# A gated encoder layer: Gelu where each block's result lies, two pairs of g_b tiles as seven products, and a DMA that makes a weight's lower part

## The chip, the cores and the metric

The kernel runs on one core of one Trainium2 chip. The metric is the time of one execution in microseconds (us) of device time. The core has five engines with instruction queues of their own that run beside each other: TensorE (PE, matrix products), VectorE (DVE), ScalarE (ACT), GpSimd (POOL) and SyncE (SP). POOL and SP also start DMA transfers from their queues. An engine takes its instructions in the order in which they stand; a waiting instruction holds up all that stand behind it.

## The reference

One layer on 512 time steps with a model width of 2048, all in float32:

```python
h = rmsnorm(x, norm_g)
v, bg, cg, za, u, zb, ga, gb = split(h @ w_in)          # widths 2048 x4, 1024 x2, 2048 x2
ya = bg * causal_depthwise_conv(cg * v, conv_w)
ya = (ya * silu(za)) @ w_out_a
yb = gelu(s5_scan(u, ...))                              # 64 groups of 16 channels, 64 states each
yb = yb * sigmoid(yb @ w_glu + b_glu)
yb = (yb * silu(zb)) @ w_out_b
m = sigmoid(ga) * ya + sigmoid(gb) * yb
out = rmsnorm(x + m @ w_o, final_g)
```

## The kernel before, in words

**Products.** Each float32 operand is held as two parts, an upper one that is rounded to the matmul's type and a lower one that is the rest; both stand in one tile `pair` for activations, in `w_hi` and `w_lo` for weights. A weight tile is 128 x 1024: eight blocks of 128 rows for 128 output columns. `gemm` (lines 828 to 836) takes one such tile and, for each block, issues three matmuls of 512 columns (lines 833 to 835): upper by upper, upper by lower, lower by upper. `hgemm` is two of them, one output tile of 128 channels by 512 steps over all 2048 rows.

**Seven products.** `seven` (lines 1082 to 1111) computes a pair of output tiles with seven products over half the rows in place of eight, from sums of weight blocks (`add7`) and sums of activations (`h_comb`). A product is 8 matmuls of 512 columns with `w_hi` (line 1073) and 8 of 256 with `w_lo` (line 1078). Of its seven weight tiles five are loaded by SP; on two of these a second load of POOL adds another block by an accumulating DMA (line 647), and two sums are DVE operations (lines 567 and 571).

**The stream of weights.** `WStream` holds a list of weight tiles in the order of use. For each, SP loads `w_raw` (line 641), ACT makes `w_hi` by a cast (`_hi`, line 663) and DVE makes `w_lo` as `w_raw - w_hi` (`_lo`, line 680). There are four buffers of `w_hi` and four of `w_lo`; `get`, called at each product, prepares those a few products ahead.

**Stages.** First u (8 tiles, with the norm). Then the gate stage: 16 g_b tiles (`gate`: a `hgemm`, Tanh on ACT, a store to `gb_d` on POOL's queue) and 8 z_b tiles, and beside them the SSM. Then GLU (8 gemms on the Gelu operands `yg`), the product with w_out_b (16 gemms; there the stored g_b tiles come back and are multiplied with the result into `tb_d`), two g_a tiles, and the stage of sevens: for j = 0, 2, ..., 14 a pair each of cg, v, z_a and b_g, and for j = 2 to 12 also a pair of g_a. At the end w_out_a, the sum m and w_o.

**The SSM beside the gates.** `ssm_blocks` is a generator over four blocks of 8 x 2 groups. Each yields pieces of work: `loads` (15 DMAs on POOL's queue: u, b and c, a broadcast table, another table), `front`, `table`, `pe1` (matmuls), `post`, `scan`, `skip`, and one block later `pe2` (matmuls) and `result` (adds the matmul's result to `ysb`, and stores it by four DMAs over u in the tile `uy`). Behind it in the list of background work stands `gelu`, which for each of eight slabs of `uy` copies it, makes the Gelu in its Tanh form and splits it into a `pair` of `yg`.

**What sets the order.** A planner, `step(n)`, is called in each gemm with a rate (5.3 in the gate stage): it takes pieces from the background list until their estimated cost has used up n. A piece that yields a number above 0 lets as many following calls pass. The language's scheduler then sets the order of each engine's queue.

Of the kernel before, what the change touches and what calls it, by code (L numbers as in the profile page):

```python
# [9 lines left out]
F32 = mybir.dt.float32  # L10
# [16 lines left out]
SLOT = 1024  # L27
EPS = 1e-6
MAGIC = 12582912.0
RATE = 5.3  # L30
PRATE = 1.6
R7 = 1.2
WARM = 9
NR4 = 37
NA = 0
NAB = 2
NB7 = 14
LEAST = 0.6
# [234 lines left out]
class Block:  # L273
# [13 lines left out]
    def loads(self):  # L287
        c, nc, b, q0 = self.c, self.c.nc, self.b, self.q0
        u4 = self.u4 = self.new([P, QB, NCH], "u4")
        for s in range(T):  # L290
            nc.gpsimd.dma_start(u4[s * 32:(s + 1) * 32], self.uy[self.rows, :, s, :])
        smal = self.smal = self.new([P, QB, 2, 2, NC], "bc")
        nc.gpsimd.dma_start(smal[:, :, 0], self.be_d[b])
        nc.gpsimd.dma_start(smal[:, :, 1], self.ce_d[b])
        wb = self.wb = self.new([P, QB, 2, NP], "wb")
        sc = self.scratch.rearrange("(q g) s r p -> s g q (r p)", g=2)
        for s in range(T):
            for g2 in range(2):
                r0 = s * 32 + g2 * 16
                nc.gpsimd.dma_start(  # L300
                    wb[r0:r0 + 16].rearrange("c q r p -> c q (r p)"),
                    sc[s, g2, q0:q0 + QB, :].unsqueeze(0).to_broadcast([16, QB, 2 * NP]))
        bs = self.bs = self.new([P, QB, 2, NP], "bs")
        nc.gpsimd.dma_start(bs, self.bs_d[b])

    def front(self):
        c, nc, b, q0, msk = self.c, self.c.nc, self.b, self.q0, self.msk
# [191 lines left out]
                yield  # L499

    def result(self):
        c, nc, ysb = self.c, self.c.nc, self.ysb
        tt, ts, stt = _ew(nc)
        for half in range(2):
            y = ysb[:, half * 4:half * 4 + 4, :].rearrange("p q k -> p (q k)")
            tt(y, self.yp[half], y, ADD)
        for t_ in range(T):
            nc.gpsimd.dma_start(self.uy[self.rows, :, t_, :], ysb[t_ * 32:(t_ + 1) * 32])
        yield


def ssm_blocks(blocks):

    blocks[0].loads()
    yield 1
    for i, k in enumerate(blocks):
        yield from k.front()
        if i:
            blocks[i - 1].pe2()
            yield  # L520
        yield from k.table((4, 5))
        if i:
            yield from blocks[i - 1].result()
        k.pe1()
        yield from k.table((6,))
        yield from k.post()
        if i + 1 < len(blocks):
            blocks[i + 1].loads()
        yield from k.scan()
        yield from k.skip()  # L530
    yield 1
    blocks[-1].pe2()
    yield 1
    yield from blocks[-1].result()


class WStream:
# [12 lines left out]

        self.loads.append((len(self.ops), len(self.ops), src, box))

    def add(self, src, resident=False, first=None):
        box = {}
        self._load(src, box)
        self.ops.append((lambda: box["x"], box, resident, first))

# [108 lines left out]
    def _lo(self):  # L666
        c, nc = self.c, self.c.nc
        i = self.nb
        if i >= len(self.ops):
            return  # L670
        while self.na <= i:
            self._hi()
        self.nb += 1
        raw, hi, cuts, resident = self.hl[i]
        if resident:
            lo = c.r4.tile([P, SLOT], F32R, tag="r4", name="w_lo_r")
        else:
            lo = c.wp.tile([P, SLOT], F32R, tag="lo", bufs=4, name="w_lo")
        for a, b in zip(cuts, cuts[1:]):
            nc.vector.tensor_tensor(out=lo[:, a:b], in0=raw[:, a:b], in1=hi.bitcast(F32)[:, a:b], op=SUB)  # L680
        self.hl[i] = (hi, lo)
# [15 lines left out]
def hybrid_kernel(ctx: ExitStack, tc: tile.TileContext, xT, x, cvec, fg, wu, wu7, wabc,  # L697
# [44 lines left out]
    for j in range(NA):  # L742
        for h in range(2):
            W.add(wga[j, h])
    for j in range(KD):
        for h in range(2):
            W.add(wgb[j, h])
    for m in range(8):
        for h in range(2):
            W.add(wgz[m, 1 + h])  # L750
# [57 lines left out]
    def step(n=1.0):  # L808

        if hold[0] > 0:
            hold[0] -= 1
            return
        owed[0] += n
        while owed[0] > 0.0 and bg:
            t = SPENT[0]
            try:
                hold[0] = next(bg[0]) or 0
            except StopIteration:  # L820
                bg.pop(0)
                continue
            owed[0] -= max(SPENT[0] - t, LEAST)
            if hold[0]:
                owed[0] = 0.0
        owed[0] = min(owed[0], n)

    def gemm(ps, acts, first=True, last=True, steps=0.0):
# [106 lines left out]

    yg = []

    def gelu(a, b):
        q = []
        for m in range(a, b + 1):  # L940
            if m < b:
                y, t = tmp(), tmp()
                act.copy(y.rearrange("p (k s) -> p k s", s=T), uy[:, m].rearrange("p s k -> p k s"))
                act.activation(t, y, AF.Square, scale=0.044715 ** 0.5)
                stt(t, t, 1.0, y, ADD, MUL)
                act.activation(t, t, AF.Tanh, scale=0.7978845608028654)
                q.append((y, t))
                yield
            if m > a:
                y, t = q.pop(0)  # L950
                stt(t, t, 1.0, y, ADD, MUL)
                g = pair()
                split(g, t)
                yg.append(g)
                yield

    bg.append(ssm_blocks([Block(c, b, uy, scratch, bs_d, be_d, ce_d, dsk, msk) for b in range(NB)]))
    bg.append(gelu(0, 8))

    def hgemm(steps=0.0):  # L960
        ps = psum()
# [10 lines left out]

    for j in range(NA):
        gate(ga_d[j // 2][:, j % 2], RATE)
    for j in range(KD):
        gate(gb_d[j], RATE)
    zb = []
    for m in range(8):
# [56 lines left out]
    gq = []  # L1035

    def fetch_gb():
        if len(gq) < KD:
            t = tmp()
            nc.gpsimd.dma_start(t, gb_d[len(gq)])  # L1040
            gq.append(t)
# [5 lines left out]
    for j in range(KD):  # L1047
        ps = psum()
        gemm(ps, yb, steps=1.15)
        th = gq[j]  # L1050
        stt(th, th, 1.0, ps, ADD, MUL)
        nc.gpsimd.dma_start(tb_d[j // 2][:, j % 2], th)
        fetch_gb()
    for j in range(NA, NAB):
# [81 lines left out]
    def gate2(o, j):  # L1136
# [384 lines left out]
```

## Time and profile before

| what | us |
|---|---|
| median of 3 runs | 1655.29 |
| the runs | 1653.54, 1655.29, 2033.42 |
| the profiled execution | 1653.86 |
| its span, first to last instruction | 1652.1 |

The profile is of one execution. Its page gives for each engine the time it was busy, the chain of work that ended last, and groups of instructions by line with their mean duration in ns and the idle time ahead of them, with what ended that idle time. "PEld" is PE's loading of weights into its array. A matmul's duration in a row is longer than its place in the chain, since neighbours overlap; the pace of PE is read from the chain. A wait is named as "engine tile line <- what released it". The DMA share is the mean busy share of the core's 16 DMA engines.

### The profile page before, as it was taken

The numbers are of one execution on the slowest core, as the hardware profiler recorded it, in microseconds if no ns is written. First come the engines' busy times: TensorE is split into PE (matmuls) and PEld (weight loads), VectorE is DVE, ScalarE is ACT, GpSimd is POOL, SyncE is SP. The second block draws the span as 40 slices with busy tenths as digits, with TensorE's granted clock in tenths as the row PEclk, the third lists the DMA queues.
The fourth block names the chain that finished last, engine by engine and source line by source line (L and its number), as shares of the span: only waits on it lengthen the run. The fifth ranks groups of instructions, "written<-read, shape, count | busy, mean of one in ns | idle before, by whom it ended". The sixth has DMA issues, their size and how long they took to land.

```text
span 1652.1 us, 22757 instructions
## 1 busy us (share of the span) xinstructions
PE 1641.3 (99%) x8636; PEld 1409.8 (85%) x8636; DVE 1290.6 (78%) x1743; ACT 788.0 (48%) x1081; POOL 220.7 (13%) x347
## 2 busy tenths in 40 slices
PE   9999999999999999999999999999999999999997
PEld 7888888888888888888888888888888888888886
DVE  8997777976766687878878787787878778888497
ACT  6433455347422454545445455544555544455334
POOL 0003233200021100010000101010010221122000
PEclk9999999999999999999999999999999999999999
DMA  8323464432454577777767777777777878897683
GB/s 310 115 86 111 121 164 132 139 119 77 167 184 150 162 186 206 193 217 186 198 191 192 216 184 208 204 208 197 187 204 191 297 255 252 269 327 249 227 327 102
DMA packets 91918, 318.50 MB, mean 193 GB/s; under 512 B 11904, under 2 KB 12160, under 8 KB 91808
## 3 DMA queue, kind: packets, MB, share of 16 engines
q1 hardware_dynamic: 58752, 204.65, 35.7%
q0 software_dynamic: 32336, 111.30, 28.6%
q8 instruction: 67, 1.10, 0.3%
q10 hardware_dynamic: 720, 1.10, 0.2%
q14 instruction: 43, 0.35, 0.1%
HBM read 287.51 MB, written 25.30 MB: 189 GB/s over the span
## 4 chain that ended last, share of the span: by engine, by line
PE 98%; DVE 1%; DMA 0%; ACT 0%; SPq 0%; issue 0%; DVEq 0%
PE ps L1073 34%; PE ps L1078 18%; PE ps L835 10%; PE ps L833 10%; PE ps L834 10%; PE ps L1296 10%; PE ps L916 1%; PE ps L917 1%; PE ps L918 1%; PE ps L375 1%; PE ps L487 1%; PE ps L383 0%; PE ps L484 0%; DMA w_raw<-in_wu_dram 0%; DVE uy L66 0%; DVE o L76 0%
## 5 line engine op out<-in xcount | busy, mean ns | idle before, releaser
L663 ACT CAST w_hi<-w_raw 128x1024 fp32r<-128x1024 f32 (+2 forms) x459 | 479.1, 1045 | 666.1 <-PE ps L1073 278.2
L680 DVE TENSOR_TENSOR w_lo<-w_raw,w_hi 128x1024 fp32r<-128x1024 f32 (+2 forms) x459 | 556.1, 1213 | 182.1 <-ACT w_hi L663 178.8
L1073 PE MATMUL ps<-h_comb,w_hi 128*128 128x512 f32 x1408 | 352.6, 392 | 0.0
L1073 PEld LDWEIGHTS ps<-h_comb,w_hi 128*128 128x128 f32 x1408 | 253.2, 189 | 45.3
L835 PE MATMUL ps<-pair,w_lo 128*128 128x512 f32 x720 | 280.6, 390 | 0.7 <-DVE w_lo L680 0.7
L833 PE MATMUL ps<-pair,w_hi 128*128 128x512 f32 x720 | 280.9, 390 | 0.0
L834 PE MATMUL ps<-pair,w_hi 128*128 128x512 f32 x720 | 280.2, 389 | 0.0
L1073 PE MATMUL ps<-pair,w_hi 128*128 128x512 f32 x1056 | 264.4, 392 | 0.0
L1073 PEld LDWEIGHTS ps<-pair,w_hi 128*128 128x128 f32 x1056 | 190.1, 189 | 34.0
L1078 PEld LDWEIGHTS ps<-h_comb,w_lo 128*128 128x128 f32 x1408 | 192.1, 190 | 13.7
L1078 PE MATMUL ps<-h_comb,w_lo 128*128 128x256 f32 x1408 | 196.3, 282 | 0.0
L835 PEld LDWEIGHTS ps<-pair,w_lo 128*128 128x128 f32 x720 | 135.2, 188 | 29.2 <-DVE w_lo L680 1.4
L834 PEld LDWEIGHTS ps<-pair,w_hi 128*128 128x128 f32 x720 | 135.2, 188 | 28.0
L833 PEld LDWEIGHTS ps<-pair,w_hi 128*128 128x128 f32 x720 | 135.2, 188 | 27.7
L1078 PEld LDWEIGHTS ps<-pair,w_lo 128*128 128x128 f32 x1056 | 144.1, 190 | 10.3
L1078 PE MATMUL ps<-pair,w_lo 128*128 128x256 f32 x1056 | 147.3, 282 | 0.0
L66 DVE TENSOR_TENSOR half<-ps,half 128x512 f32<-128x512 f32 x132 | 90.6, 686 | 67.4 <-PE ps L1078 67.4
L647 POOL DMA_DIRECT2D w_raw<-in_wabc_dram x64 | 55.1, 861 | 554.9 <-DMA w_raw<-in_wabc_dram 392.2
L1296 PE MATMUL ps<-w_hi,pair 128*128 128x512 f32 x192 | 60.7, 389 | 0.0
L567 DVE TENSOR_TENSOR w_raw<-w_raw 128x1024 f32<-128x1024 f32 x44 | 53.9, 1225 | 2.2 <-DMA w_raw<-in_wga_dram 0.7
L571 DVE TENSOR_TENSOR w_raw<-w_raw 128x1024 f32<-128x1024 f32 x44 | 53.9, 1225 | 1.5
L1296 PE MATMUL ps<-w_hi,m_half 128*128 128x512 f32 x160 | 50.7, 389 | 0.0
(215 smaller groups left out, 1718.7 us busy)
## 6 DMA issues: line engine op xcount, KB each, us to landing
w_raw<-in_wabc_dram SPq DMA_DIRECT2D x160, 512.0 KB, 4.5
w_raw<-in_wga_dram SPq DMA_DIRECT2D x76, 512.0 KB, 5.1
w_raw<-in_wabc_dram POOLq DMA_DIRECT2D x64, 512.0 KB, 6.4
w_raw<-in_wo_dram SPq DMA_DIRECT2D x52, 512.0 KB, 5.9
w_raw<-in_wgb_dram SPq DMA_DIRECT2D x48, 512.0 KB, 3.5
w_raw<-in_wgz_dram SPq DMA_DIRECT2D x24, 512.0 KB, 3.3
w_raw<-in_wga_dram POOLq DMA_DIRECT2D x24, 512.0 KB, 7.2
m_r<-m POOLq DMA_DIRECT2D x32, 256.0 KB, 5.6
```

Of the source, the lines that this page charges most:

```text
L66: return v.tensor_tensor(out=o, in0=a, in1=b, op=op)
L567: tt(out=b11["x"], in0=b11["x"], in1=s1["x"], op=ADD)
L571: tt(out=s1["x"], in0=b12["x"], in1=b11["x"], op=ADD)
L647: nc.gpsimd.dma_start(box["x"], src.rearrange("p a b -> p (a b)"), accum_op=ADD)
L663: nc.scalar.copy(hi[:, a:b], raw[:, a:b])
L680: nc.vector.tensor_tensor(out=lo[:, a:b], in0=raw[:, a:b], in1=hi.bitcast(F32)[:, a:b], op=SUB)
L833: nc.tensor.matmul(ps, hi[:, k], a[:, 0], start=first and k == 0, stop=False)
L834: nc.tensor.matmul(ps, hi[:, k], a[:, 1], start=False, stop=False)
L835: nc.tensor.matmul(ps, lo[:, k], a[:, 0], start=False, stop=last and k == 7)
L1073: nc.tensor.matmul(ps if flat else both, hi[:, k], a, start=first and k == 0, stop=False, skip_group_check=True)
L1078: nc.tensor.matmul(ps[:, HL:], lo[:, k], a[:, :HL] if flat else a[:, 0], start=False, stop=last and k == 7, skip_group_check=True)
L1296: nc.tensor.matmul(ps, l, r[:, k2, c0:c1], start=first and k2 == i == 0, stop=last and k2 == 1 and i == 2, skip_group_check=True)
```

## The change

There are four parts.

1. `WStream.add` takes `by_dma`; for the second weight tile of each g_b output tile ACT writes `-w_hi` into `w_lo` and POOL's queue starts a DMA that adds the weight from memory, in place of DVE's subtraction.
2. The g_b tiles 12 to 15 leave the gate stage. In the w_out_b stage their results are stored as they are, and after the sevens of j = 0 and j = 14 `seven` computes the pairs 12, 13 and 14, 15; `gate_b` loads the stored pair, multiplies and stores it.
3. `Block.result` makes the Gelu on its 1024 columns, in three pieces, before the store; `gelu` becomes `operands`, which only makes the pairs. The rate is 6.0, and the last block's pieces yield -1: they end the surplus that a call has left, without letting calls pass.
4. `loads` and the stores of `result` are started on SP's queue.

```diff
-RATE = 5.3
+RATE = 6.0
+NGB = 12
+GB7 = {0: 12, 14: 14}
...
     def loads(self):
-            nc.gpsimd.dma_start(u4[s * 32:(s + 1) * 32], self.uy[self.rows, :, s, :])
+            nc.sync.dma_start(u4[s * 32:(s + 1) * 32], self.uy[self.rows, :, s, :])
...
     def result(self):
-        for half in range(2):
-            y = ysb[:, half * 4:half * 4 + 4, :].rearrange("p q k -> p (q k)")
-            tt(y, self.yp[half], y, ADD)
+        y = self.ysb.rearrange("p q k -> p (q k)")
+        for half in range(2):
+            h = y[:, half * L:(half + 1) * L]
+            tt(h, self.yp[half], h, ADD)
+        t = self.new([P, QB * NCH], "gelu")
+        nc.scalar.activation(t, y, AF.Square, scale=0.044715 ** 0.5)
+        yield
+        stt(t, t, 1.0, y, ADD, MUL)
+        nc.scalar.activation(t, t, AF.Tanh, scale=0.7978845608028654)
+        yield
+        stt(y, t, 1.0, y, ADD, MUL)
         for t_ in range(T):
-            nc.gpsimd.dma_start(self.uy[self.rows, :, t_, :], ysb[t_ * 32:(t_ + 1) * 32])
+            nc.sync.dma_start(self.uy[self.rows, :, t_, :], self.ysb[t_ * 32:(t_ + 1) * 32])
...
-    yield 1
-    blocks[-1].pe2()
-    yield 1
-    yield from blocks[-1].result()
+    yield -1
+    blocks[-1].pe2()
+    yield -1
+    yield from blocks[-1].result()
+    yield 1
...
     def _lo(self):
+        if "src" in self.ops[i][1]:
+            nc.scalar.mul(lo, hi.bitcast(F32), -1.0)
+            nc.gpsimd.dma_start(lo, self.ops[i][1]["src"].rearrange("p a b -> p (a b)"), accum_op=ADD)
+            cuts = cuts[:1]
...
-    for j in range(KD):
+    for j in range(NGB):
         for h in range(2):
-            W.add(wgb[j, h])
+            W.add(wgb[j, h], by_dma=h == 1)
...
+        if j in GB7:
+            i = GB7[j]
+            W.add7(wgb[i, 0], wgb[i + 1, 0], wgb[i + 1, 1], wgb[i, 1])
...
                 hold[0] = next(bg[0]) or 0
+                if hold[0]:
+                    owed[0] = min(owed[0], 0.0)
...
-            if hold[0]:
-                owed[0] = 0.0
...
-    def gelu(a, b):
...
+    def operands():
+        for m in range(8):
+            g = pair()
+            v = uy[:, m].rearrange("p s k -> p k s")
+            act.copy(g[:, 0].rearrange("p (k s) -> p k s", s=T), v)
+            tt(g[:, 1].rearrange("p (k s) -> p k s", s=T), v,
+               g[:, 0].bitcast(F32).rearrange("p (k s) -> p k s", s=T), SUB)
+            yg.append(g)
+            yield
...
-        th = gq[j]
-        stt(th, th, 1.0, ps, ADD, MUL)
+        if j < NGB:
+            th = gq[j]
+            stt(th, th, 1.0, ps, ADD, MUL)
+        else:
+            th = tmp()
+            act.copy(th, ps)
...
+    def gate_b(o, j):
+        t, r = wide("tz"), wide("tb_w")
+        nc.gpsimd.dma_start(r, tb_d[j // 2])
+        act.activation(t, o, AF.Tanh, scale=0.5)
+        yield
+        stt(r, t, 1.0, r, ADD, MUL)
+        nc.gpsimd.dma_start(tb_d[j // 2], r)
+        yield
...
+        if j in GB7:
+            bg.append(gate_b(seven("gb", hb), GB7[j]))
```

How this moves instructions is seen at three places. The first is the start of the gate stage on POOL's queue. Before, stores of g_b tiles (L970) and the loads of the first block (L291 to L304) stand there:

```order
L970 DMA gb_112<-tmp 128x512
L970 DMA gb_113<-tmp 128x512
L291 DMA ssm_u_1336<-uy 32x8x128 x4
L970 DMA gb_114<-tmp 128x512
L293 DMA ssm_bc<-in_be_dram 128x8x32
L268 DMA ssm_scr<-ssm_wn 64x512
```

Now a load onto `w_lo` (L698) follows each store, each store now being L985:

```order
L698 DMA w_lo<-in_wgb_dram 128x1024 x2
L985 DMA gb_112<-tmp 128x512
L698 DMA w_lo<-in_wgb_dram 128x1024
L985 DMA gb_113<-tmp 128x512
L698 DMA w_lo<-in_wgb_dram 128x1024
L271 DMA ssm_scr<-ssm_wn 64x512
L985 DMA gb_114<-tmp 128x512
L698 DMA w_lo<-in_wgb_dram 128x1024
```

The accumulating loads stand behind the stores of earlier tiles, and the block's loads are gone from this queue.

The second place is SP's queue over the gate stage and what follows. Before, nothing but weight loads stands there (wgb holds g_b and w_out_b, wgz GLU and z_b, wabc and wga those of the sevens):

```order
L641 DMA w_raw<-in_wgb_dram 128x1024 x32
L641 DMA w_raw<-in_wgz_dram 128x1024 x24
L641 DMA w_raw<-in_wgb_dram 128x1024 x16
L641 DMA w_raw<-in_wga_dram 128x1024 x4
L641 DMA w_raw<-in_wabc_dram 128x1024 x40
```

Now, around the third block's loads and the first block's result (`uy<-ssm_y`, L520):

```order
L658 DMA w_raw<-in_wgb_dram 128x1024 x8
L294 DMA ssm_u_2069<-uy 32x8x128 x3
L520 DMA uy<-ssm_y 32x8x128 x4
L294 DMA ssm_u_2069<-uy 32x8x128
L296 DMA ssm_bc<-in_be_dram 128x8x32
L297 DMA ssm_bc<-in_ce_dram 128x8x32
L303 DMA ssm_wb<-ssm_scr 16x8x128 x8
L307 DMA ssm_bs<-in_bs_dram 128x1024
L658 DMA w_raw<-in_wgz_dram 128x1024 x7
```

The 15 loads and the four stores stand between two groups of weight loads.

The third place is ACT's queue at the end of the gate stage, where GLU's operands are made. Before, copies of u (L943), the Gelu's two functions (L944, L946) and the casts of the pairs (L734) mix with the casts of weights (L663):

```order
L943 COPY tmp<-uy 128x512
L944 ACTIVATE tmp<-tmp 128x512
L943 COPY tmp<-uy 128x512
L663 CAST w_hi<-w_raw 128x1024
L946 ACTIVATE tmp<-tmp 128x512
L944 ACTIVATE tmp<-tmp 128x512
L943 COPY tmp<-uy 128x512
L946 ACTIVATE tmp<-tmp 128x512
L734 CAST pair<-tmp 128x512
```

Now the last block's Gelu (L513, L516) stands two weight casts ahead of eight casts straight from u (L966):

```order
L513 ACTIVATE ssm_gelu<-ssm_y 128x1024
L516 ACTIVATE ssm_gelu<-ssm_gelu 128x1024
L680 CAST w_hi<-w_raw 128x1024
L998 ACTIVATE tmp<-ps 128x512
L680 CAST w_hi<-w_raw 128x1024
L966 CAST pair<-uy 128x512 x8
L998 ACTIVATE tmp<-ps 128x512
```

Of the work that follows the last result, the two functions for each slab are gone. On PE, 71 matmuls (23 of a z_b gemm under way and two whole gemms) stand in the new order between the last SSM matmul and the first GLU matmul.

More of the change, by code (lines that the diff above doesn't have):

```diff
@@ L290, in loads @@
         for s in range(T):
-            nc.gpsimd.dma_start(u4[s * 32:(s + 1) * 32], self.uy[self.rows, :, s, :])
+            nc.sync.dma_start(u4[s * 32:(s + 1) * 32], self.uy[self.rows, :, s, :])
         smal = self.smal = self.new([P, QB, 2, 2, NC], "bc")
-        nc.gpsimd.dma_start(smal[:, :, 0], self.be_d[b])
-        nc.gpsimd.dma_start(smal[:, :, 1], self.ce_d[b])
+        nc.sync.dma_start(smal[:, :, 0], self.be_d[b])
+        nc.sync.dma_start(smal[:, :, 1], self.ce_d[b])
         wb = self.wb = self.new([P, QB, 2, NP], "wb")
@@ L299, in loads @@
                 r0 = s * 32 + g2 * 16
-                nc.gpsimd.dma_start(
+                nc.sync.dma_start(
                     wb[r0:r0 + 16].rearrange("c q r p -> c q (r p)"),
@@ L303, in loads @@
         bs = self.bs = self.new([P, QB, 2, NP], "bs")
-        nc.gpsimd.dma_start(bs, self.bs_d[b])
+        nc.sync.dma_start(bs, self.bs_d[b])
     def front(self):
@@ L501, in result @@
     def result(self):
[L502 removed]
+        c, nc = self.c, self.c.nc
         tt, ts, stt = _ew(nc)
+        y = self.ysb.rearrange("p q k -> p (q k)")
         for half in range(2):
[L505 to L506 removed]
+            h = y[:, half * L:(half + 1) * L]
[7 more added lines that the diff above has]
+        stt(y, t, 1.0, y, ADD, MUL)
         for t_ in range(T):
[L508 removed]
+            nc.sync.dma_start(self.uy[self.rows, :, t_, :], self.ysb[t_ * 32:(t_ + 1) * 32])
         yield
@@ L517, in ssm_blocks @@
         yield from k.front()
+        res = iter(())
         if i:
@@ L520, in ssm_blocks @@
             yield
+            res = blocks[i - 1].result()
         yield from k.table((4, 5))
-        if i:
-            yield from blocks[i - 1].result()
+        next(res, None)
         k.pe1()
-        yield from k.table((6,))
+        for _ in k.table((6,)):
+            yield
+            next(res, None)
         yield from k.post()
@@ L551, in _load, with add @@
         self.loads.append((len(self.ops), len(self.ops), src, box))
-    def add(self, src, resident=False, first=None):
-        box = {}
+    def add(self, src, resident=False, first=None, by_dma=False):
+        box = {"src": src} if by_dma else {}
         self._load(src, box)
@@ L936, in hybrid_kernel @@
     yg = []
-    def gelu(a, b):
[L939 to L955, printed above, removed]
+    def operands():
[7 more added lines that the diff above has]
+            yield
     bg.append(ssm_blocks([Block(c, b, uy, scratch, bs_d, be_d, ce_d, dsk, msk) for b in range(NB)]))
-    bg.append(gelu(0, 8))
+    bg.append(operands())
     def hgemm(steps=0.0):
@@ L974, in hybrid_kernel @@
         gate(ga_d[j // 2][:, j % 2], RATE)
-    for j in range(KD):
+    for j in range(NGB):
         gate(gb_d[j], RATE)
@@ L1037, in fetch_gb @@
     def fetch_gb():
-        if len(gq) < KD:
+        if len(gq) < NGB:
             t = tmp()
@@ L1140, in gate2 @@
         yield
+    def gate_b(o, j):
[5 more added lines that the diff above has]
+        nc.gpsimd.dma_start(tb_d[j // 2], r)
+        yield
     hb = blocks(hp, th7)
```

## The prediction

> **What bounds the kernel.** I read the page first, then the waits of TensorE, the chain of waits, then each stage by windows. Times are microseconds (us). Busy time of each engine and the chain's shares, from the page:
>
> ```profile
> PE 1641.3 (99%) x8636; PEld 1409.8 (85%) x8636; DVE 1290.6 (78%) x1743; ACT 788.0 (48%) x1081; POOL 220.7 (13%) x347
> ...
> PE 98%; DVE 1%; DMA 0%; ACT 0%; SPq 0%; issue 0%; DVEq 0%
> ```
>
> A modelled busy share of 99% does not yet say that nothing waits, so the second view is what TensorE (PE) waited for, total, times, longest:
>
> ```profile
> PE ps L791 <- DVE bgl L785: 1.1, 1, 1.1
> PE ps L835 <- DVE w_lo L680: 0.7, 1, 0.7
> PE ps L916 <- ACT pair L893: 0.4, 1, 0.4
> ```
>
> That is 2.2 us in the whole execution. The change can win only what it takes out of PE's own matmuls, and lose only by making PE wait. The two stages it touches, the gate stage (g_b and z_b tiles with the SSM beside them) and the stage of seven products, by windows:
>
> ```profile
> core 0: us, PE busy (x) PEld busy (x) DVE busy (x) ACT busy (x) POOL busy (x), PEclk, DMA share, GB/s
> 95.00:403.00 308.00, 307.31 (x1608) 260.66 (x1607) 243.53 (x426) 143.04 (x240) 67.92 (x113) 1.00 0.42 124
> ...
> 554.00:1034.00 480.00, 480.00 (x2749) 422.36 (x2748) 372.75 (x380) 243.87 (x292) 47.68 (x59) 1.00 0.73 198
> ```
>
> VectorE (DVE) is at 79% and 78%, the granted clock is 1.00: PE paces both, and the others have room.
>
> **The one term of the sum: PE.** The price of a product in each form is read off the chain of waits, where the same piece comes round (start, length):
>
> ```profile
> 98.05 0.23 PE ps L835
> ...
> 113.69 0.23 PE ps L835
> ...
> 557.12 1.84 PE ps L1073 x8
> ...
> 1031.99 1.84 PE ps L1073 x8
> ```
>
> The first two rows are 23 groups of three matmuls apart: 15.64 / 23 = 0.68, so one weight tile of eight groups (a gemm) takes 5.44 and a tile of two gemms 10.88. The last two are 170 products apart: 474.87 / 170 = 2.793, so a pair of tiles by seven products takes 19.55. Removed: four g_b tiles, 4 x 10.88 = 43.5. Added: two sevens, 2 x 19.55 = 39.1. PE gains 4.4. The SSM's own matmuls and those on w_out_b are as many as before.
>
> **Work that leaves or joins the other engines in the gate stage.** That stage gets 43.5 shorter, 308.0 to 264.5, so its cover must be counted again. Groups of that window (busy, mean ns of one):
>
> ```profile
> L663 ACT CAST w_hi<-w_raw 128x1024 fp32r<-128x1024 f32 x46 | 48.1, 1050 | 92.8 <-PE ps L834 73.6 <-issue 14.8 <-DVE ssm_wide L76 4.4
> ...
> L969 ACT ACTIVATE tmp<-ps 128x512 f32<-128x512 f32 x16 | 9.5, 595 | 47.6 <-PE ps L835 47.5
> L943 ACT COPY tmp<-uy 128x512 f32<-128x512 f32 x8 | 9.0, 1131 | 5.0 <-DMA uy<-ssm_y 5.0
> ...
> L944 ACT ACTIVATE tmp<-tmp 128x512 f32<-128x512 f32 x8 | 5.0, 628 | 0.1
> ```
>
> And of DVE, in the window from 92 to 372:
>
> ```profile
> L680 DVE TENSOR_TENSOR w_lo<-w_raw,w_hi 128x1024 fp32r<-128x1024 f32 x46 | 55.6, 1219 | 30.9 <-ACT w_hi L663 30.9
> L66 DVE TENSOR_TENSOR ssm_h<-ssm_h,ssm_rr 128x1024 f32<-128x1024 f32 x16 | 19.2, 1220 | 0.1
> ...
> L66 DVE TENSOR_TENSOR ssm_y<-ps,ssm_y 128x512 f32<-128x512 f32 x8 | 5.2, 685 | 2.0 <-PE ps L487 2.0
> ...
> L66 DVE TENSOR_TENSOR uy<-ps,ss 128x512 f32<-128x512 f32 x4 | 3.9, 1042 | 0.0
> ```
>
> DVE loses 12 subtractions to the DMA and 8 with the four tiles: 20 x 1.22 = 24.4. The old Gelu had three operations on each of eight slabs (8 x 3 x 0.69 = 16.6); the new one has two of 1024 columns on each of four blocks (8 x 1.22 = 9.8) and eight subtractions that read the strided u (I take 1.04, the row with a strided operand: 8.3). DVE: 243.5 - 24.4 - 16.6 + 18.1 = 220.6 of 264.5, or 83%. ScalarE (ACT) gains 12 negated copies (12.6) and loses eight casts (8.4); its Gelu goes from three operations of 0.63 on eight slabs (15.1) to two of 1.05 on four blocks (8.4): 143.0 + 12.6 - 8.4 - 15.1 + 8.4 = 140.5, or 53%. The higher RATE only decides how early that work is put between the gemms; where it came to stand is in the order, and I count from there. What DVE waits for there, beside its own queue:
>
> ```profile
> DVE w_lo L680 <- ACT w_hi L663: 27.0, 9, 5.5
> DVE ssm_t L66 <- DMA gb<-tmp: 5.2, 1, 5.2
> DVE ssm_rr L66 <- ACT ssm_rr L428: 3.2, 3, 1.1
> DVE zb L76 <- ACT tmp L983: 3.2, 1, 3.2
> DVE ssm_t L66 <- ACT ssm_sl L363: 2.8, 3, 0.9
> ```
>
> The 27.0 are waits for a cast that itself waits for PE to release a buffer: DVE is ahead there. The other 14.4 stay, and 220.6 + 14.4 = 235.0 is still 29 below 264.5. Price: nothing; the cover is those 29.
>
> **The DMA that makes w_lo.** The trace has no such DMA on a w_lo tile. The nearest is the accumulating DMA of the sevens, of the same 512 KB from POOL's queue (issue to landing, median), with POOL's time for one and for a store of a g_b tile (min/median/max, ns):
>
> ```profile
> w_raw<-in_wabc_dram POOLq DMA_DIRECT2D x64, 512.0 KB, 6.4
> ...
> w_raw<-in_wga_dram POOLq DMA_DIRECT2D x24, 512.0 KB, 7.2
> ```
>
> ```profile
> L647 POOL DMA_DIRECT2D w_raw<-in_wga_dram x24: 848/868/937, 694.6 to 1453.1; - x24
> ```
>
> ```profile
> L970 POOL DMA_DIRECT2D gb<-tmp x16: 539/562/688, 110.2 to 299.2; - x16
> ```
>
> In POOL's order it stands behind the store of the tile before, which waits for PE and a Tanh. From the end of that tile: Tanh 0.6, store 0.6, issue 0.9, landing 7.2: 9.3. The weights of three gemms lie between, 3 x 5.44 = 16.3. Bounds: nothing while it lands within 14.2; 12 times the excess beyond. I take nothing, since both rows lie well under 14.2, and were taken at a DMA share of 0.73 against 0.42 here. A gain is excluded: DVE's subtraction cost PE 0.7 in all.
>
> **SSM loads and results on SP's queue.** POOL loses 60 load and 16 store issues, SP gets them, between weight loads. Issues of the gate stage, median to landing:
>
> ```profile
> w_raw<-in_wgb_dram SPq DMA_DIRECT2D x22, 512.0 KB, 3.4
> ...
> ssm_u<-uy POOLq DMA_DIRECT2D x16, 128.0 KB, 3.0
> ssm_wb<-ssm_scr POOLq DMA_DIRECT2D x32, 64.0 KB, 5.9
> ssm_bs<-in_bs_dram POOLq DMA_DIRECT2D x4, 512.0 KB, 4.6
> uy<-ssm_y POOLq DMA_DIRECT2D x16, 128.0 KB, 3.4
> ssm_bc<-in_be_dram POOLq DMA_DIRECT2D x4, 128.0 KB, 5.3
> ssm_bc<-in_ce_dram POOLq DMA_DIRECT2D x4, 128.0 KB, 6.9
> ```
>
> A block's 15 loads are 512 + 256 + 512 + 512 KB, 3.5 weight loads: 3.5 x 3.4 = 11.9 ahead of the next weight. A cast waits mostly for PE's release three gemms before use (73.6 in its row above), not for its load: 16.3 less 1.05 and 1.22 leaves 14.0. Price nothing, with 2.1 to spare plus whatever the load was early. The stores of a result wait on SP for DVE's last Gelu operation, and the weight loads behind them wait too; in the new order the last store has two such loads behind it, for the third and fourth gemm after GLU's start, which is time enough.
>
> By the Trainium skill (DMA: Bandwidth & Descriptors, SWDGE vs HWDGE vs iDMA) each DMA engine has separate internal queues for the two kinds of issuer and goes round them, so what left POOL's queue for SP's now stands in line with the weights instead of sharing with them. The trace of before cannot show that; it is the mechanism of rival 2.
>
> **The end of the stage.** Before, Gelu followed as eight slabs; now only copy and subtraction are left behind the last block's result. In the new order 71 matmuls stand on PE between the last SSM matmul and the first that needs a Gelu operand: 71 x 0.2267 = 16.1, and the eighth operand is due 7 x 0.68 = 4.8 later, at 20.9. The chain: sum 0.69, Square 1.05 (as a 1024 cast), 1.22, Tanh 1.05, 1.22, store to u 3.4, eight copies of 1.13, a subtraction 1.04: 18.7. It is hidden, by 2.2. The landing of that store, min/median/max, says how firmly:
>
> ```profile
> DMA to landing us min/median/max: 2.4/3.4/8.1
> ```
>
> At 8.1 the last operand comes at 23.4, 2.5 late (rival 1).
>
> **Later stages.** The two new sevens bring ten loads on SP and four accumulating ones on POOL, as each of the 44 sevens before did without a wait of PE, in place of eight loads, four stores and four loads back of g_b tiles. A g_b pair after the sevens of j=0 and j=14 adds a Tanh, one DVE operation of 1.22 and a load and store of 512 KB. DVE has 107 idle of 480 there; the j=14 one also gives the last out_a more cover. The four plain copies in the w_out_b stage replace operations as long. Nothing.
>
> **Sum.** The profiled execution took 1653.9 (1652.1 span), 1.4 under the median 1655.3 shown. 1653.9 - 4.4 = 1649.5; I say 1650.
>
> **Rivals.**
> 1. The last store lands late: 1649.5 + 2.5 = 1652. For: the slowest landing before was just this last store. Against: weight loads stood around it, and in the new order the next ones come behind it.
> 2. Weights starve behind SP's queue (ends slower than before). SP's longest wait for a released buffer, in its waits:
>
> ```profile
> SPq L641 <- DVE ssm_h L66: 53.3, 4, 17.1
> ```
>
> If a block's loads meet such a wait, the weight is 17.1 + 11.9 = 29.0 late against 14.0: 15 for each of three blocks, 1664.5 for one, 1694.5 for all. It makes the kernel slower from a delay of 14.0 + 4.4 / 3 = 15.5 at each block. Against: before, weights met that wait and PE lost 0.7 in all. By the skill's rule of one line for both, the 11.9 counts in full, which is how I counted it.
> 3. The accumulating DMA lands beyond 14.2: at three times 7.2 it costs 12 x 7.4 = 89, 1738. Nothing in the rows speaks for that.
>
> **Chances.** Forecast 0.66, rival 1 0.20, rival 2 0.10 (0.07 at one block, 0.03 at all), rival 3 0.02, a shorter time than the sum explains 0.02. Range: from 1647.5 (the sum less the 1.8 between the two close runs of before) to 1660, between rival 1 and one block of rival 2; it leaves out about 0.18. Two per cent, 33 us, is about what a measurement of this kernel can tell from no change: faster than that 0.01, for PE has no 33 us to lose; slower 0.04 (rival 3 and most of rival 2 at all blocks); within it 0.95.
>
> **What would show it.** Right: groups of L857 to L859 at 656 each, 46 sevens of 19.55, PE's waits still near 2 us, the gate stage near 264 long. Rival 1 shows as a PE wait of about 2.5 for the pair tiles at the first GLU gemm; rival 2 as waits of w_hi for w_raw's DMA followed by PE waits at each block; rival 3 as PE waits for the DMA into w_lo. It is wrong if PE's waits exceed 10 us.

## The result, and the profile after

The changed kernel takes 1664.99 us, the median of four runs (1663.09 to 1665.65), against 1654.41 before: a ratio of 1.0065, interval 1.0049 to 1.0081. One of the four executions of the kernel before, a slow one of 2033.42, is not in the ratio. The changed kernel is slower, by less than the two per cent, and outside the predicted range of 1647.5 to 1660. It is near to what rival 2 gave for one block, 1664.5; that is chance, for PE waits for weights no longer than before (0.7). The profiled execution took 1665.65 with a span of 1663.6. Its page and its view of TensorE's waits (total, times, longest), to be held against those quoted in the prediction:

```profile
PE 1641.6 (99%) x8668; PEld 1411.0 (85%) x8668; DVE 1296.1 (78%) x1741; ACT 807.4 (49%) x1093; POOL 187.5 (11%) x283
...
PE 88%; DVE 6%; DMA 3%; issue 2%; ACT 1%; POOL 0%; DVEq 0%; POOLq 0%; ACTq 0%
```

```profile
PE ps L378 <- ACT ssm_sl L366: 7.1, 5, 2.8
PE ps L490 <- DVE ssm_h L69: 1.4, 1, 1.4
PE ps L1092 <- ACT half L1107: 1.3, 1, 1.3
...
PE ps L857 <- DVE ssm_y L69: 0.9, 1, 0.9
...
PE ps L859 <- DVE w_lo L701: 0.7, 1, 0.7
```

TensorE (PE) is still called 99% busy, since its busy time is modelled, but the chain that ended last gives it 88% instead of 98%. (The chain steps aside to what released PE; the other 12% are not idle time. The waits add up to 13.3 us, against 2.2 before.) The waits are at the SSM's own products: L378 is `pe1`, whose weights `ssm_sl` ScalarE (ACT) copies in L366, and L490 is `pe2`. How long each stage is, from the starts of PE's matmuls (in both kernels some 9 us follow behind the last one):

| stage | before, us | after, us | predicted change | measured |
|---|---|---|---|---|
| start to the first g_b tile | 95.1 | 94.4 | 0 | -0.7 |
| gate stage (g_b, z_b, SSM) | 306.6 | 276.9 | -43.5 | -29.7 |
| GLU, w_out_b, first ga tiles | 152.5 | 152.6 | 0 | +0.1 |
| sevens from j=0 to 14 | 743.0 | 782.1 | +39.1 | +39.1 |
| last ga tiles, plain w_out_a | 65.3 | 65.3 | 0 | 0 |
| sevens of w_out_a | 117.3 | 120.0 | 0 | +2.7 |
| w_o to PE's last matmul | 163.4 | 163.4 | 0 | 0 |

The two sevens cost what was counted, to a tenth. The gate stage lost 13.8 of its 43.5, and the sevens of w_out_a another 2.7. The gate stage by windows:

```profile
94.00:371.00 277.00, 266.94 (x1410) 226.20 (x1409) 223.28 (x399) 137.41 (x225) 30.47 (x44) 0.99 0.53 138
```

VectorE (DVE) worked 223.28 and ACT 137.41, where the prediction had 220.6 and 140.5. The sums were right, and DVE has over 50 us to spare. What went wrong is seen in the order of time at the first block, in PE's timeline (start, length):

```profile
149.58 0.39 PE L859 MATMUL ps<-pair,w_lo 128*128 128x512 f32 x1
152.81 2.85 PE L378 MATMUL ps<-ssm_u,ssm_sl 128*128 128x128 f32 x16 [2.85 <-ACT ssm_sl L366]
156.64 3.78 PE L378 MATMUL ps<-ssm_u,ssm_sl 128*128 128x128 f32 x16 [0.97 <-ACT ssm_sl L366]
```

and in ACT's at the same place:

```profile
150.00 0.60 ACT L984 ACTIVATE tmp<-ps 128x512 f32<-128x512 f32 x1 [1.94 <-PE ps L859]
150.49 1.04 ACT L680 CAST w_hi<-w_raw 128x1024 fp32r<-128x1024 f32 x1
151.43 1.33 ACT L366 ACTIVATE ssm_sl<-ssm_t,cvec_t 128x512 f32<-128x512 f32 x2
```

`pe1` stands directly behind the last matmul of a g_b tile. The copy that makes its weights stands on ACT behind the Tanh of that same tile (L984), which needs that last matmul, and behind a weight cast. PE waits for 0.60 + 1.04 + 0.7, and the hand-overs between. Before, the same piece of ACT's and of PE's timeline read:

```profile
150.68 0.60 ACT L969 ACTIVATE tmp<-ps 128x512 f32<-128x512 f32 x1 [9.56 <-PE ps L835]
151.17 1.99 ACT L663 CAST w_hi<-w_raw 128x1024 fp32r<-128x1024 f32 x2
153.05 1.34 ACT L363 ACTIVATE ssm_sl<-ssm_t,cvec_t 128x512 f32<-128x512 f32 x2
```

```profile
156.82 0.39 PE L834 MATMUL ps<-pair,w_hi 128*128 128x512 f32 x1
157.05 1.95 PE L375 MATMUL ps<-ssm_u,ssm_sl 128*128 128x128 f32 x16
```

The copy is no earlier there (153.05 against 151.43), but one more gemm stood between the tile's end and `pe1`, and covered it. RATE 6.0 put `pe1` behind the 10th gemm of the stage, the end of a tile, instead of a quarter into the 12th, and the blocks some seven gemms apart instead of eight. In the second block `pe1` stands behind the 17th gemm, in the middle of a tile, and does not wait. In the third it stands directly behind `pe2` of the second, without a gemm between, and waits again:

```profile
206.04 1.95 PE L378 MATMUL ps<-ssm_u,ssm_sl 128*128 128x128 f32 x16
256.39 2.05 PE L378 MATMUL ps<-ssm_u,ssm_sl 128*128 128x128 f32 x16 [1.03 <-ACT ssm_sl L366]
260.22 2.05 PE L378 MATMUL ps<-ssm_u,ssm_sl 128*128 128x128 f32 x16 [1.78 <-ACT ssm_sl L366]
```

The first copy starts at 255.00, just when the last `ssm_u` by `ssm_mi` product of `pe2` ends (254.92). That the copy waits for `pe2` is seen in ACT's waits of the kernel before already, where a gemm between covered it:

```profile
ACT ssm_sl L363 <- PE ps L484: 11.5, 3, 3.8
```

### The profile page after: what moved, and what is told of

It is laid out like the page before. It is cut to its first block, busy times and chain, and to the rows that moved or that the text cites. A ratio compares the mean times of both kernels' runs of the same rounds, so it can differ in the third digit from the quotient of the medians.

```text
span 1663.6 us, 22862 instructions
## 1 busy us (share of the span) xinstructions
PE 1641.6 (99%) x8668; PEld 1411.0 (85%) x8668; DVE 1296.1 (78%) x1741; ACT 807.4 (49%) x1093; POOL 187.5 (11%) x283
## 4 chain that ended last, share of the span: by engine, by line
PE 88%; DVE 6%; DMA 3%; issue 2%; ACT 1%; POOL 0%; DVEq 0%; POOLq 0%; ACTq 0%
PE ps L1092 35%; PE ps L1097 18%; PE ps L1326 9%; PE ps L857 7%; PE ps L858 7%; PE ps L859 7%; DMA h_sum<-yag 1%; DVE w_lo L701 1%; PE ps L941 1%; PE ps L940 1%; PE ps L942 1%; DMA w_raw<-in_wga_dram 1%; DVE ssm_t L69 1%; DVE tmp L79 1%; PE ps L490 1%
## 5 line engine op out<-in xcount | busy, mean ns | idle before, releaser
L680 ACT CAST w_hi<-w_raw 128x1024 fp32r<-128x1024 f32 (+2 forms) x465 | 485.1, 1044 | 656.9 <-PE ps L1092 283.7
L701 DVE TENSOR_TENSOR w_lo<-w_raw,w_hi 128x1024 fp32r<-128x1024 f32 (+2 forms) x453 | 548.8, 1212 | 178.5 <-ACT w_hi L680 175.2
L1092 PE MATMUL ps<-h_comb,w_hi 128*128 128x512 f32 x1472 | 368.8, 392 | 2.1 <-ACT half L1107 1.3
L1092 PEld LDWEIGHTS ps<-h_comb,w_hi 128*128 128x128 f32 x1472 | 264.7, 189 | 49.9 <-ACT half L1107 1.5
L1092 PE MATMUL ps<-pair,w_hi 128*128 128x512 f32 x1104 | 276.4, 392 | 0.0
L857 PE MATMUL ps<-pair,w_hi 128*128 128x512 f32 x656 | 255.8, 390 | 0.9 <-DVE ssm_y L69 0.9
L859 PE MATMUL ps<-pair,w_lo 128*128 128x512 f32 x656 | 255.4, 390 | 0.7 <-DVE w_lo L701 0.7
L858 PE MATMUL ps<-pair,w_hi 128*128 128x512 f32 x656 | 255.4, 390 | 0.0
L1092 PEld LDWEIGHTS ps<-pair,w_hi 128*128 128x128 f32 x1104 | 198.7, 189 | 35.6
L1097 PEld LDWEIGHTS ps<-h_comb,w_lo 128*128 128x128 f32 x1472 | 200.8, 190 | 14.4
L1097 PE MATMUL ps<-h_comb,w_lo 128*128 128x256 f32 x1472 | 205.3, 282 | 0.0
L1097 PE MATMUL ps<-pair,w_lo 128*128 128x256 f32 x1104 | 153.9, 282 | 0.0
L857 PEld LDWEIGHTS ps<-pair,w_hi 128*128 128x128 f32 x656 | 123.1, 188 | 26.3 <-PE ps L386 1.0
L858 PEld LDWEIGHTS ps<-pair,w_hi 128*128 128x128 f32 x656 | 123.2, 188 | 25.9 <-DVE pair L69 0.4
```

What stands on the lines that cost most here:

```text
L680: nc.scalar.copy(hi[:, a:b], raw[:, a:b])
L857: nc.tensor.matmul(ps, hi[:, k], a[:, 0], start=first and k == 0, stop=False)
L858: nc.tensor.matmul(ps, hi[:, k], a[:, 1], start=False, stop=False)
L859: nc.tensor.matmul(ps, lo[:, k], a[:, 0], start=False, stop=last and k == 7)
L1092: nc.tensor.matmul(ps if flat else both, hi[:, k], a, start=first and k == 0, stop=False, skip_group_check=True)
L1097: nc.tensor.matmul(ps[:, HL:], lo[:, k], a[:, :HL] if flat else a[:, 0], start=False, stop=last and k == 7, skip_group_check=True)
```

## The experiments

Two theories stood first: Q, the wait of SyncE's (SP's) queue for the scratch store holds up the weights behind it; P, at the new pace SSM products stand too early on PE for the engines that make their operands. Others are stated where they begin; a "product" of the stage there is a gemm, half a tile. The table gives what all showed; "lost" is what the gate stage and GLU took beyond the 306.6 and 43.7 of the kernel before, with 10.88 less for each tile that is gone (306.6 for 24 tiles, 284.9 for 22, 263.1 for 20). The kernel before had a median of 1653.9 to 1654.9 beside each.

| run | RATE | tiles | lost, us | time, us | ratio to before, interval |
|---|---|---|---|---|---|
| changed kernel | 6.0 | 20 | 13.9 | 1665.0 | 1.0065, 1.0049 to 1.0081 |
| a1 SSM transfers on GpSimd | 6.0 | 20 | 13.3 | 1665.5 | 1.0071, 1.0056 to 1.0086 |
| a2 lower parts on DVE | 6.0 | 20 | 13.8 | 1666.5 | 1.0084, 1.0068 to 1.0101 |
| a3 no g_b sevens | 6.0 | 24 | 12.1 | 1667.5 | 1.0087, 1.0070 to 1.0104 |
| a4 old pace | 5.3 | 20 | 24.8 | 1677.6 | 1.0144, 1.0129 to 1.0159 |
| b1 old pace, no g_b sevens | 5.3 | 24 | -0.2 | 1655.4 | 1.0006, 0.9996 to 1.0015 |
| b2 before, pace alone | 6.0 | 24 | 8.8 | 1661.7 | 1.0043, 1.0028 to 1.0058 |
| b3 before, sevens alone | 5.3 | 20 | 25.1 | 1676.4 | 1.0132, 1.0117 to 1.0147 |
| b4 two ga tiles early | 5.3 | 22 | 5.6 | 1664.0 | 1.0052, 1.0035 to 1.0069 |
| c1 store early | 6.0 | 20 | 14.1 | 1667.6 | 1.0074, 1.0061 to 1.0087 |
| c2 one pair | 5.5 | 22 | 0.1 | 1657.7 | 1.0023, 1.0014 to 1.0031 |
| c3 one pair, store early | 5.5 | 22 | 0.6 | 1656.5 | 1.0011, 1.0003 to 1.0020 |
| d1 one product between | 7.4 | 20 | 23.1 | 1673.6 | 1.0115, 1.0098 to 1.0132 |
| e1 the same, lower parts on DVE | 7.4 | 20 | 10.2 | 1665.4 | 1.0060, 1.0046 to 1.0074 |
| e2 one pair, Gelu in the block | 5.5 | 22 | 2.6 | 1655.5 | 1.0007, 0.9998 to 1.0016 |

**One part taken back each (a1 to a4).** All four are edits of the changed kernel. a1 puts the SSM's transfers back:

```diff
-            nc.sync.dma_start(u4[s * 32:(s + 1) * 32], ...
+            nc.gpsimd.dma_start(u4[s * 32:(s + 1) * 32], ...
```

> The changed kernel with the SSM loads and the stores of the results back on POOL's queue. Theory Q (SP's queue): the first block's table loads wait on SP for the scratch store and hold the weight loads behind them, so that the first SSM products wait 4.2 us and then run about 2.7 us longer at a lower clock; then this run is about 7 us faster than the changed kernel, near 1658, with no PE wait at the first SSM products. Theory P (pace): the SSM products stand too early in PE's queue for DVE and ACT; then the first wait stays and the time is within 2 us of 1665.

SP's wait for the scratch store, in its view of waits after the change,

```profile
SPq L303 <- DMA ssm_scr<-ssm_wn: 29.8, 1, 29.8
```

has no row in a1, and the time is the same, so Q's 7 us did not come. The case against Q is not made by a1 alone, though: there PE's gaps at the first block, 3.2 and 1.4, shrank to one of 2.6, and against that stood new waits of 2.1 for the accumulating DMAs and 0.9 more in GLU. In c1 below SP's wait is cut by two thirds and PE's stays. a2 lets DVE subtract every lower part again:

```diff
-            W.add(wgb[j, h], by_dma=h == 1)
+            W.add(wgb[j, h])
```

> The changed kernel with DVE's subtraction for all lower weight parts of g_b, no accumulating DMA there. DVE gets 12 x 1.22 = 14.6 us more work in the gate stage. Theory P: DVE is short of time where the SSM products wait, so PE's waits grow by part of that, 1666 to 1675. Theory Q: the waits come from SP's queue, which is the same, so 1665 within 2 us. If the accumulating DMA itself is what holds something, the time falls below 1663.

The stage took 276.8 again, so the accumulating DMA neither costs nor wins there, and DVE is not short of time there. (The profile is of an execution of 1663.8; the others took 1664.7 to 1670.2. The median lies in the ranges of both theories.) a3 keeps all sixteen g_b tiles in the stage:

```diff
-NGB = 12
+NGB = 16
-GB7 = {0: 12, 14: 14}
+GB7 = {}
```

> The changed kernel with all 16 g_b tiles in the gate stage and no g_b pairs among the sevens (the rest as changed). PE's own work grows by 4.4 us. Theory Q or P: the SSM products stand behind the same gemms as in the changed kernel, so PE's waits in the gate stage stay at about 13 us; the waits of 2.7 us in the sevens of w_out_a go if the g_b pairs cause them: 1667 with that, 1669 without. If the shorter gate stage is itself the cause, the time falls to 1656 to 1660.

The stage still loses 12.1, with four more tiles to hide the SSM beside: a shorter stage is not what makes these waits. Nor do the g_b pairs make the loss in the sevens of w_out_a, for without them it was still 2.3; that the time is the expected 1667 is luck. a4 sets RATE back and nothing else:

```diff
-RATE = 6.0
+RATE = 5.3
```

> The changed kernel with the planner's rate at 5.3 as before. The SSM products then stand 1 to 4 gemms (5 to 22 us) later on PE. Theory P: the waits at the SSM products go, 8 to 13 us faster than the changed kernel, 1652 to 1657, unless the end of the SSM then comes too late for GLU. Theory Q: the weights still wait behind the scratch store on SP; only what the later place of the first products hides is won, at most 7 us, 1658 or more.

It is 12.6 us slower than the changed kernel. P had named this only as its exception. Its waits show the other half of the matter:

```profile
PE ps L857 <- ACT pair L966: 11.4, 1, 11.4
PE ps L490 <- DVE ssm_h L69: 5.1, 2, 4.9
```

The waits at `pe1` are gone (0.4 left), but now the last block ends too late: its `pe2` is behind the 40th and last gemm, and GLU's first product waits 11.4 for the pairs (L966) made from its result.

**The pace by itself (b1, b2).** b1 is a3 with RATE 5.3; b2 is the kernel before with RATE 6.0 and nothing else:

> The changed kernel with RATE back at 5.3 and all sixteen g_b tiles in the gate stage; Gelu in the block, SyncE's queue and the accumulating DMA stay. It differs from the run without the sevens (a3, gate stage 318.9 us, 12.3 more than before) in RATE alone. Theory P (pace: at 6.0 units a product the SSM's products reach TensorE before VectorE and ScalarE have made their operands): the gate stage is 306.6 us within 1.5 and the time 1654 to 1657. Theory G (the Gelu that was put into each block delays the next block, whatever the pace): the stage stays at 315 to 320 and the time at 1663 to 1668.

> The kernel before with RATE 6.0 instead of 5.3 and nothing else. P: waits of the SSM's products as in the changed kernel, gate stage 314 to 319 us, time 1662 to 1667. G: no waits, time within 2 us of 1654.

The stage took 306.5 and 315.6: both as P had it, G falls as the main cause. In b1 no wait in the gate stage is left but the 0.7 that before had too. The waits of b2:

```profile
PE ps L375 <- ACT ssm_sl L363: 5.3, 3, 3.8
```

RATE alone brings 9.0 of the 12.3 that a3's stage grew by; the other 3.3, with the Gelu in the block, the new step code and the DMAs, were not taken apart.

**The sevens by themselves (b3)**: the kernel before with NGB, GB7, `gate_b` and the plain copies, as in the change's diff.

> The kernel before with the four g_b tiles moved to two sevens and nothing else: RATE 5.3, Gelu behind the last block, GpSimd's queue for the loads. The stage has 40 products, and in the kernel before the last SSM product starts behind the 42nd. P: the SSM does not end before the last z tile; GLU's first product waits for it, the stage ends some 25 us later than its 263 us of products, that is at about 385 us of the trace, and the time is 1670 to 1680. If the four tiles could simply be taken out, as the prediction on record counted: 1650 within 2.

GLU's first product ended its wait at 377.9, 7 us sooner than I had put it, but the sevens alone lose 25.1 in stage and GLU, and the time is in the expected range:

```profile
PE ps L838 <- ACT pair L736: 18.8, 4, 17.6
```

So the four tiles were what the SSM was hidden beside. Taken out at the old pace, the end is waited for; with RATE raised to end in time, the products on the way.

**Giving the stage tiles back (b4).** The ga tiles behind w_out_b are moved ahead of the g_b tiles:

```diff
-RATE = 6.0
+RATE = 5.3
-NA = 0
+NA = 2
-        gemm(ps, yb, steps=1.15)
+        gemm(ps, yb, steps=2.2)
```

> The changed kernel with RATE 5.3 and the first two ga tiles, which stood behind the w_out_b products, put ahead of the g_b tiles (NA 2; the rows of steps in the w_out_b products raised from 1.15 to 2.2 units to carry the sums that the ga tiles had carried). The stage then has 44 products instead of 40, at the old pace. P: the stage is 284.9 us plus 0 to 6, the two sevens keep their 4.4 us, time 1649 to 1656. G: 12 us of waits stay, time 1660 to 1664.

The stage lost 3.0 and GLU 2.6, as P said; yet its time was missed by 8. (The time is at the edge of G's range, but G's 12 us of waits are not in the stage.) The sevens that now follow w_out_b directly took 5.4 more, with waits of PE for `half` tiles at 542 and 556 us, and those of w_out_a lost 3.8. So the ga tiles had most likely been cover themselves; the raised steps in the w_out_b products were not tested apart.

**An earlier first block, and one pair (c1, c2, c3).** c1 moves the lines that compute `ssm_wn`, and its store, ahead of the angle tables.

> The changed kernel with the SSM's weight table (ssm_wn, the tile that goes to the scratch store) computed ahead of the angle tables and the base powers instead of behind them; same instructions, pace 6.0, forty products. In the changed kernel the store lands at 132 us of the trace and TensorE waits 3.2 and 1.4 us at the first block's products, with some 2.7 us more at a lower clock behind them. Theory S (the SSM starts too late: its first block hangs on the round trip of the scratch store): these 7 us go, the gate stage is 268 to 271 us instead of 276.9, the time 1656 to 1660. Theory W (the pace is too fast inside the blocks, and what is won at the first block is waited for at the next ones): the waits behind 250 us grow, the gate stage stays at 274 to 277 and the time at 1663 to 1666.

The store was issued at 111.6 instead of 129.9, SP's wait for it fell from 29.8 to 9.9, and PE's gap ahead of `pe1` stayed at 3.24 from start to start: S falls, and with it Q's account of the first block. (The stage, 277.1, and the time lie just above W's ranges, and the later waits hardly grew.) DVE's timeline shows that the data was ready, the first copy's operand at 142.33:

```profile
141.65 0.68 DVE L69 TENSOR_TENSOR ssm_t<-ssm_t 128x512 f32<-128x512 f32 x1
...
144.40 0.48 DVE L69 TENSOR_TENSOR ssm_ft<-ssm_ft 128x128 f32<-128x128 f32 x2
153.94 0.69 DVE L69 TENSOR_TENSOR ssm_t<-ssm_wb,ssm_bs 128x512 f32<-128x512 f32 x1 [9.06 <-ACT ssm_sl L366]
```

and ACT's, why nothing came of it:

```profile
151.15 0.60 ACT L984 ACTIVATE tmp<-ps 128x512 f32<-128x512 f32 x1 [4.61 <-PE ps L859]
151.64 1.04 ACT L680 CAST w_hi<-w_raw 128x1024 fp32r<-128x1024 f32 x1
152.58 1.33 ACT L366 ACTIVATE ssm_sl<-ssm_t,cvec_t 128x512 f32<-128x512 f32 x2
```

ACT stood idle for 4.61, because the Tanh ahead of the copy waits for the tile that PE was on. This wait, the first block's, is made by the order alone. c2 moves one pair at a pace between the two:

```diff
-RATE = 6.0
+RATE = 5.5
-NGB = 12
+NGB = 14
-GB7 = {0: 12, 14: 14}
+GB7 = {14: 14}
```

> The changed kernel with one pair of g_b tiles moved instead of two (NGB 14, GB7 {14: 14}) and RATE 5.5: the stage has 44 products, 284.9 us without waits, and the one seven saves 2.2 us. The last SSM product at RATE 5.3 stood behind the 42nd product, at 6.0 behind the 37th, so here behind the 40th or 41st, 16 to 22 us ahead of GLU, where the changed kernel needed 23 and had no wait. Theory P (pace and room decide): waits of 1 to 6 us together in the stage and at GLU, time 1653 to 1659, so no gain. If one pair fits without waits: 1650 to 1653.

> As the run with one pair (c2), with the SSM's weight table ahead of the angle tables as in c1. Theory S: the first block has its operands in time, stage 285 to 288, time 1651 to 1655 and 1 to 4 under c2. Theory W: within 1 of c2.

```profile
94.60:379.40 284.80, 284.06 (x1505) 241.47 (x1504) 226.14 (x402) 145.88 (x233) 33.32 (x48) 1.00 0.55 148
```

In c2 the stage has no wait left beyond those of the kernel before, so up to the sevens of w_out_a 2.1 of the 2.2 of one pair were there. P's time came out, its waits did not. The sevens of w_out_a lost 4.2 (c3: 4.8), and both kernels are slower than before. c3 took 1.2 less than c2, at the edge of what S said, but the time is above S's range and the two intervals overlap: not decided.

**One product between (d1, e1).** d1 is the changed kernel with a held-back step, and a RATE that still ends the SSM behind the 36th gemm:

```diff
-RATE = 6.0
+RATE = 7.4
...
+        yield 1
         k.pe1()
```

> The changed kernel with one product held back ahead of the first SSM products of each block (a yield of 1 ahead of pe1) and RATE 7.4, so that the SSM is not handed out more slowly: the last SSM products stand behind the 36th product instead of the 37th, and no longer is a block's first product issued in the same gap between two products as the ScalarE copy that makes its weights. Theory O (order: the copy stands on ScalarE behind the tanh and the weight rounding of the tile that has just ended, so TensorE waits for it whenever both fall into one gap): the waits at pe1, 3.2 + 1.4 and 1.3 + 2.1 us, fall to under 1 us each, and the stage to 265 to 271 us. Theory T (throughput: VectorE and ScalarE cannot do the SSM in 37 products, whatever the order): waits of 10 us or more stay in the stage, at pe1, at pe2 or at GLU, and it stays at 273 to 281.

Neither theory had 286:

```profile
PE ps L860 <- DMA w_lo<-in_wgb_dram: 9.6, 3, 5.8
PE ps L378 <- ACT ssm_sl L366: 5.3, 4, 1.6
```

The longest wait at `pe1` fell from 2.8 to 1.6, but at 7.4 units a gemm the negated copies came later on ACT (GpSimd waited 23.1 for six of them between 160 and 250 us), and so did the accumulating DMA that follows each. e1 takes those DMAs away:

> The run with one product held back (d1) with every lower weight part of the g_b tiles subtracted on VectorE again, no accumulating DMA. In d1 TensorE waited 9.6 us in 3 waits for the accumulating DMA and 5.3 for the SSM's copies, and the stage took 286 us where its products are 263. Theory O (order): without those DMAs the 9.6 us go and nothing takes their place, the stage is 268 to 277 us, under that of the changed kernel. Theory T (throughput: the SSM handed out in 36 products asks more of VectorE and ScalarE than they have): the subtraction now stands behind the SSM's work on VectorE and TensorE waits for it or for the SSM, the stage is 278 to 288.

```profile
94.30:368.00 273.70, 265.18 (x1412) 223.91 (x1411) 236.78 (x412) 127.69 (x214) 20.72 (x33) 1.00 0.40 122
```

273.1, in O's range and outside T's, and 3.8 under the changed kernel's stage; DVE carried 13.5 more than in the changed kernel, and this did no harm. But the profile is of the execution of 1660.9 and the other three took 1664.6 to 1666.4, so that the whole gained nothing, and the 3.8 may not be there in each. And 10 us stay, 5.1 of them at `pe1`. The edit did not put a gemm where it was meant to: in the new order `pe1` of the second and third block starts directly behind `pe2` again, and in the first two matmuls behind the end of a tile.

```profile
203.19 0.61 PE L490 MATMUL ps<-ssm_h,ssm_el 128*128 128x127 f32 x4
204.83 1.38 PE L378 MATMUL ps<-ssm_u,ssm_sl 128*128 128x128 f32 x10 [1.03 <-ACT ssm_sl L366]
```

So order is part of the price; whether it is all of it, neither run shows.

**The sevens of w_out_a (d2, e2).** d2 is the kernel before again; e2 is c2 without the accumulating DMAs and with GpSimd's queue.

> The kernel before, unchanged, for a second profile. The changed kernels lost 1.1 to 4.8 us in the sevens of w_out_a, with the same code there as before, where the profile of before shows none. If this is the spread of that stage: one to three us there in this profile too. If it comes from the change: none again.

> The run with one pair moved at RATE 5.5 (c2) without the accumulating DMAs and with the SSM's loads and results on GpSimd's queue as before, so that the Gelu in the block and one pair of g_b tiles as a seven are all that is left of the change. The gate stage and the sevens together come 2.2 us under the kernel before, as in c2. If the loss at the w_out_a sevens (4.2 us in c2) belongs to the queue or the accumulating DMA: it falls to about 1 and the time to 1652 to 1654, under both kernels. If it belongs to neither: 1655 to 1658 again.

```profile
PE ps L1073 <- DVE half L66: 0.4, 1, 0.4
```

This is d2's only wait in that stage; it lost 0.8 there against the first profile, at 1654.29 (ratio 0.9999, 0.9989 to 1.0008). Kernels made from before lost 0 to 1.7 there (b3 most), those made from the changed one 1.1 to 4.8, e2 2.1, with the code of the stage unchanged. So neither the DMAs nor the queue explain all of it. What PE waits behind can be seen in the changed kernel and in c2: ACT or DVE stands for a DMA's landing, and the operation on `half` that PE needs stands behind in its queue. The costliest of ACT's waits for DMAs in this stage, of before, d2, the changed kernel and c2:

```profile
ACT w_hi L663 <- DMA w_raw<-in_wga_dram: 2.5, 1, 2.5
ACT w_hi L663 <- DMA w_raw<-in_wga_dram: 10.2, 3, 4.0
ACT w_hi L680 <- DMA w_raw<-in_wga_dram: 10.5, 4, 4.4
ACT pair L755 <- DMA m_r<-m: 4.2, 1, 4.2
```

The first two rows are of the same kernel, so these waits differ from execution to execution, and d2 had the wait of 10.2 and lost only 0.8. Why they cost the changed kernels more, one profile of each doesn't settle; open. In e2 the expected 2.2 less did not come either: gate stage and GLU lost 2.6. b1 and e2 can't be told from the kernel before. No version beat it.

## Why the prediction was wrong

- **The term of the sum** (tiles out, sevens in) was right: 39.1 of 39.1 in the sevens, and c2's stage is 21.8 shorter for two tiles, as 2 x 10.88 says.
- **The failed step** is the cover of the gate stage: "220.6 + 14.4 = 235.0 is still 29 below 264.5. Price: nothing; the cover is those 29." Ahead of it stood that the higher RATE "only decides how early that work is put between the gemms". Where it is put is the price. The SSM is a chain from DVE and ACT to PE and back, and PE takes its products in a fixed order; idle time of DVE elsewhere in the stage does not shorten a wait at one place. Moving the whole stage to RATE 6.0 costs 9.0 by itself (b2), and leaving RATE at 5.3 costs 25 with four tiles gone (b3, a4), most of it at the end, and nothing with all of them there (b1). The 13.8 lost are some 10.9 of gaps between PE's starts, and 2.9 of matmuls at a lower clock behind them.
- **The order was read at three places** and not at the one that decided: where `pe1` stands against the Tanh and the copy. In the changed kernel's trace no gemm stands between them.
- **SP's queue** (rival 2): the wait that was counted, 17.1 for a buffer, was not the longest; one of 29.8 for the scratch store, which had not been counted, came. PE waited 0.7 for weights, as before. The rival's sign was there once: ACT waited 5.3 for a weight's load ahead of the first block's `pe1`, but then stood idle for 1.9 before the Tanh, so PE's wait does not come from it. With SP's wait at 9.9 (c1) or gone (a1) the time did not fall. The prediction's "nothing" holds as far as these runs show.
- **The accumulating DMA** (rival 3): landed in a median of 6.6 and at most 7.1, within the 14.2, and cost nothing at RATE 6.0 (a2). That it can be late is shown by d1, at another pace.
- **The end of the stage** (rival 1): GLU took 43.8 against 43.7; hidden as counted.
- **Later stages**: "Nothing" was right but for the sevens of w_out_a, 2.7 in the profile. PE's waits there stand behind waits of ACT and DVE for a DMA; why these cost the changed kernels more stays open.
- The text said that it is wrong if PE's waits exceed 10 us; the view after adds up to 13.3. The 0.18 that its range was to leave out is not the sum of its own chances, which give 0.14 (rivals 2 and 3, and the shorter time).

## What to carry to other kernels

Work that is hidden beside a stage has a length of its own: before taking products out of the stage, ask where the hidden chain ends at its present pace, and price the tail or the faster pace, not the engines' idle sums. When a pace is raised, look in the order for products that come to stand directly behind the tile whose epilogue the operand's maker queues behind; in the first block of before, b1 and c2 about one gemm between was cover enough. And test a pace on the old kernel by itself: one number changed in b2 showed two thirds of the loss.

## What the runs showed of the hardware

PE's clock falls behind gaps shorter than I had expected to matter. After the gap ahead of the first block's `pe1`, 3.0 beyond the regular 0.23, in the windows of the changed kernel:

```profile
150.00:160.00 10.00, 6.21 (x31) 5.92 (x32) 5.62 (x15) 9.00 (x17) 3.46 (x6) 0.69 0.59 124
160.00:170.00 10.00, 10.00 (x67) 8.38 (x67) 6.24 (x10) 7.82 (x14) 0.77 (x1) 0.97 0.82 143
```

The granted clock was 0.69, and from 154.0 to 160.0 the SSM's matmuls started 0.213 apart instead of 0.112: with what followed some 2.9 us more. The same first-block gap (3.0 to 4.9) cost 1.7 to 3.1 so in a2, a3, b2 and c1; one of 2.2 in a3 cost 2.2. In the sevens of w_out_a of c2 one of 2.1 cost 1.7:

```profile
1470.00:1480.00 10.00, 8.57 (x38) 7.39 (x39) 7.65 (x9) 4.42 (x5) 1.06 (x2) 0.83 0.92 319
```

Two gaps of 2.2 and 2.4 in b4 cost nothing, one of 2.5 at the first block of a1 0.3, and gaps up to 1.9 at most 0.6 where none longer stood just ahead. The Trainium skill (TensorE: Matmul & The Clock Gate, HAM oscillation — how this bites in real kernels) asks for no idle gap above about 3.4 us; here somewhat shorter ones already cost, so the measurement decides, though not each time.
